# A small first piece of a pooling kernel moved from partitions 0–29 to partitions 64–93

## The chip, the cores and the metric

One core of one Trainium2 chip. The metric is the device time of one execution in microseconds (us). The granted clock was 1.0 throughout. A run also gives a profile of one execution, whose span is about 1.8 us shorter than its time.

## The reference

Pooling with exponent 2 over windows of four along the last axis, float32:

```python
x: (32, 256, 4096), p = 2, kernel_size = 4
result[b, c, i] = sqrt(mean(abs(x[b, c, 4*i : 4*i+4]) ** 2))      # (32, 256, 1024)
```

134.2 MB are read and 33.6 MB written, with one square, three quarters of an add and a quarter of a root per element between. It is a matter of moving data.

## The kernel before

The input is one flat row of numbers. Most of it goes through in 20 big tiles of 128 partitions (up to 13,184 numbers each) in three input slots. ScalarE squares in place, VectorE sums fours into one of two output buffers, ScalarE takes the root, and the result is stored (the last tiles differ a little). What the big tiles do not cover, 840 x 128 numbers, is the small piece: 30 partitions of 3,584 numbers. It is loaded first, into the second output buffer, which is not needed yet.

```python
    Q = 30
    odd = ODD * P // Q                       # 840 * 128 // 30 = 3584
    t = o_tiles[1][0:Q, 0:odd]
    nc.sync.dma_start(out=t, in_=xf[(total - ODD) * P:total * P].rearrange("(p w) -> p w", p=Q))
    ahead = 0
    while ahead < n and loads[ahead][0] < X_SLOTS:
        load(ahead)                          # the first three big tiles, on the same queue
        ahead += 1
    nc.vector.tensor_tensor(out=t, in0=t, in1=t, op=mybir.AluOpType.mult)
    o = o_tiles[1][0:Q, odd:odd + odd // k]
    nc.vector.tensor_reduce(out=o, in_=t.rearrange("p (n j) -> p n j", j=k), ...)
    nc.scalar.activation(out=o, in_=o, func=Act.Sqrt, scale=1.0 / k)
    stores["odd"] = nc.scalar.dma_start(out=..., in_=o)
    ...
    for i in range(n):                       # then tile by tile, shortened
        # load(ahead) as soon as the sums have freed a slot (SyncE's queue)
        # ScalarE: square in place; VectorE: sums; ScalarE: root of an earlier group; store
```

## Time and profile before

| | before |
|---|---|
| median of 3 executions | 393.93 us (393.88 to 394.1) |
| span of the profiled execution | 393.3 us |
| busy, VectorE / ScalarE | 274.5 / 275.4 us (70% each) |
| moved | 167.77 MB, 427 GB/s over the span |

In profile lines ACT is ScalarE and DVE is VectorE; SPq and ACTq are the queues of SyncE and ScalarE, from which loads and stores are issued; xt are the input slots, ot the output buffers.

How to read it: two engines at 70% and data movement at 9 tenths or more in nearly every slice mean that the DMA engines set the time. The lines are in the prediction.

### The profile page before, as it was taken

To read this page: it belongs to the slowest core of one execution; us is meant where nothing else is said; L and a number is where in the kernel's file an instruction comes from. 1 tells how busy PE (TensorE), PEld (TensorE's weight loads), DVE (VectorE), ACT (ScalarE), POOL (GpSimd) and SP (SyncE) were. 2 spreads that over 40 slices of the span, in tenths; PEclk is the share of its full clock that TensorE was granted. 3 is DMA by queue.
4 is the path that set the end of the run, shared out by engine and by line. 5 is a ranking of instruction groups with operands and counts; after the bars stand their busy time and mean duration, and the time that the engine had idled before them with its cause. 6 is when DMAs were issued, how large, how long until landed. Compare 5 with 4: busy or idle time off the path is not lost.

```text
span 393.3 us, 182 instructions
## 1 busy us (share of the span) xinstructions
DVE 274.5 (70%) x36; ACT 275.4 (70%) x38; POOL 0.2 (0%) x4
## 2 busy tenths in 40 slices
DVE  4207898885869376948693869396929690989991
ACT  1095879919990899099809991998099809986991
POOL 0000000000000000000000000000000000000000
DMA  8999999999989999999999999999999899999996
GB/s 312 429 440 429 467 445 451 381 432 469 434 386 429 472 429 429 456 402 429 429 432 426 429 472 429 456 400 467 429 437 429 386 429 467 429 429 423 440 409 295
DMA packets 4554, 167.77 MB, mean 427 GB/s; under 512 B 526, under 2 KB 526, under 8 KB 556
## 3 DMA queue, kind: packets, MB, share of 16 engines
q1 hardware_dynamic: 3501, 144.04, 85.0%
q10 hardware_dynamic: 1053, 23.73, 14.0%
HBM read 134.22 MB, written 33.55 MB: 427 GB/s over the span
## 4 chain that ended last, share of the span: by engine, by line
DMA 54%; ACT 25%; DVE 19%; SPq 0%; issue 0%; ACTq 0%
DMA xt<-in_x_dram 54%; ACT xt L167 22%; DVE ot L111 14%; DVE xt L122 3%; ACT ot L102 3%; DVE ot L124 1%; DVE xt L124 1%; ACT xt L102 1%; SPq L82 0%; ACTq L99 0%; SPq L132 0%
## 5 line engine op out<-in xcount | busy, mean ns | idle before, releaser
L167 ACT ACTIVATE xt<-xt 128x13184 f32<-128x13184 f32 (+4 forms) x23 | 217.4, 9458 | 97.9 <-DMA xt<-in_x_dram 96.2
L111 DVE TENSOR_REDUCE ot<-xt 128x3296 f32<-128x13184 f32 x15 | 208.3, 13886 | 88.7 <-ACT xt L167 88.7
L102 ACT ACTIVATE ot<-ot 128x6592 f32<-128x6592 f32 x9 | 51.1, 5679 | 0.0
L122 DVE TENSOR_TENSOR xt<-xt 128x3296 f32<-128x3296 f32 (+5 forms) x9 | 34.5, 3834 | 16.9 <-ACT xt L167 16.8
L124 DVE TENSOR_TENSOR ot<-xt 128x3296 f32<-128x3296 f32 (+1 forms) x4 | 10.9, 2733 | 0.1
L143 ACT ACTIVATE ot<-ot 30x896 f32<-30x896 f32 x1 | 0.9, 948 | 10.8 <-DVE ot L139 10.8
L137 DVE TENSOR_TENSOR ot<-ot 30x3584 f32<-30x3584 f32 x1 | 3.9, 3880 | 5.0 <-DMA ot<-in_x_dram 5.0
L124 DVE TENSOR_TENSOR xt<-xt 128x1448 f32<-128x1448 f32 (+4 forms) x5 | 7.0, 1409 | 0.2
L102 ACT ACTIVATE xt<-xt 128x3296 f32<-128x3296 f32 (+3 forms) x4 | 5.8, 1445 | 1.1 <-DVE xt L124 1.1
L164 DVE TENSOR_TENSOR xt<-xt 128x5792 f32<-128x5792 f32 x1 | 6.2, 6184 | 0.0
L139 DVE TENSOR_REDUCE ot<-ot 30x896 f32<-30x3584 f32 x1 | 3.9, 3874 | 0.0
L143 ACT ACT_TABLE_LOAD x1 | 1.3, 1283 | 0.7 <-PEq L200 0.7
L200 POOL MEMSET const-bfloat16-1.0<- 128x1 bf16 x1 | 0.1, 101 | 0.0
L200 POOL MEMSET const-uint8-127<- 128x1 uint8 x1 | 0.1, 101 | 0.0
L200 POOL MEMSET const-float32-0.0<- 128x1 f32 x1 | 0.1, 98 | 0.2 <-issue 0.2
L200 POOL MEMSET const-float32-1.0<- 128x1 f32 x1 | 0.1, 98 | 0.0
## 6 DMA issues: line engine op xcount, KB each, us to landing
xt<-in_x_dram SPq DMA_DIRECT2D x19, 6592.0 KB, 31.6
out_dram<-ot ACTq DMA_DIRECT2D x7, 3296.0 KB, 27.4
out_dram<-ot SPq DMA_DIRECT2D x2, 3296.0 KB, 24.0
xt<-in_x_dram SPq DMA_DIRECT2D x1, 5404.0 KB, 24.1
out_dram<-xt SPq DMA_DIRECT2D x1, 1648.0 KB, 11.0
out_dram<-xt SPq DMA_DIRECT2D x1, 1351.0 KB, 6.6
ot<-in_x_dram SPq DMA_DIRECT2D x1, 420.0 KB, 4.2
out_dram<-ot ACTq DMA_DIRECT2D x1, 105.0 KB, 8.7
```

The costliest lines, as they stand in the source:

```text
L102: r = nc.scalar.activation(out=o, in_=o, func=Act.Sqrt, scale=1.0 / k)
L111: r = nc.vector.tensor_reduce(out=o, in_=v.rearrange("p (n j) -> p n j", j=k), axis=mybir.AxisListType.X, op=add,)
L122: r = nc.vector.tensor_tensor(out=h, in0=q[:, :, 0:2], in1=q[:, :, 2:4], op=add)
L124: r = nc.vector.tensor_tensor(out=o, in0=h[:, :, 0], in1=h[:, :, 1], op=add)
L137: nc.vector.tensor_tensor(out=t, in0=t, in1=t, op=mybir.AluOpType.mult)
L139: nc.vector.tensor_reduce(out=o, in_=t.rearrange("p (n j) -> p n j", j=k), axis=mybir.AxisListType.X, op=mybir.AluOpType.add,)
L143: nc.scalar.activation(out=o, in_=o, func=Act.Sqrt, scale=1.0 / k)
L164: r = nc.vector.tensor_tensor(out=v, in0=v, in1=v, op=mybir.AluOpType.mult)
L167: r = nc.scalar.activation(out=v, in_=v, func=Act.Square)
L200: nc = _bacc.Bacc("TRN2", target_bir_lowering=False, num_devices=1)
```

## The change

The intent is to see whether the time depends on which partitions of the on-chip memory the small piece is loaded to. Only its place moves; bytes, instructions and waits stay.

```diff
-    Q = 30
+
+    LOW, Q = 64, 30
     odd = ODD * P // Q
-    t = o_tiles[1][0:Q, 0:odd]
+    t = o_tiles[1][LOW:LOW + Q, 0:odd]
     ...
-    o = o_tiles[1][0:Q, odd:odd + odd // k]
+    o = o_tiles[1][LOW:LOW + Q, odd:odd + odd // k]
```

## The prediction

> **What bounds the kernel now.** I read the page's slices first, then the chain that ended last, then a table of DMA traffic by stage, then the start of the timeline.
>
> Slices of the page (40 equal slices, busy tenths; GB/s moved):
>
> ```profile
> DVE  4207898885869376948693869396929690989991
> ACT  1095879919990899099809991998099809986991
> DMA  8999999999989999999999999999999899999996
> ```
>
> The DMA row is at 9 in nearly every slice, and only the first and the last slice fall clearly short. The two compute engines have 70% each and idle in between. The chain by line says the same:
>
> ```profile
> DMA 54%; ACT 25%; DVE 19%; SPq 0%; issue 0%; ACTq 0%
> DMA xt<-in_x_dram 54%; ACT xt L167 22%; DVE ot L111 14%; DVE xt L122 3%; ACT ot L102 3%; DVE ot L124 1%; DVE xt L124 1%; ACT xt L102 1%; SPq L82 0%; ACTq L99 0%; SPq L132 0%
> ```
>
> It names squares and sums as well, because a load may only be issued when the sums have freed its slot. But a load then takes 30 us and more to land, since two other tiles are queued ahead of it, so the engines that move data are never short of work. By stage (columns: busy us and instructions of each engine, clock, DMA share, GB/s):
>
> ```profile
> 0.00:5.00 5.00, 0.04 (x1) 1.28 (x1) 0.20 (x4) 1.00 0.82 255
> 5.00:13.00 8.00, 7.71 (x2) 0.22 (x1) 0.00 (x0) 1.00 0.98 422
> 94.00:300.00 206.00, 143.07 (x12) 150.03 (x17) 0.00 (x0) 1.00 1.00 434
> 345.00:370.00 25.00, 23.18 (x9) 19.88 (x5) 0.00 (x0) 1.00 1.01 434
> 370.00:394.00 24.00, 14.56 (x8) 14.76 (x7) 0.00 (x0) 1.00 0.84 359
> ```
>
> 434 GB/s is the plateau. The trace's packet records agree: a row of 52,736 B takes 1.947 us at the median, 27.09 GB/s, and 16 of those are 433.4 GB/s. All 167.77 MB at that rate are 387.1 us. The shortfall at the two ends, expressed in time at 434 GB/s, is 5.0 x (434 - 255) / 434 = 2.1 us at the start and 24 x (434 - 359) / 434 = 4.1 us at the end. 387.1 + 2.1 + 4.1 = 393.3 us, which is the span. So only some 6 us of the run are not full-rate traffic, and the change stands in the first 2 of them.
>
> The small piece in the timeline:
>
> ```profile
> 0.73 0.45 SPq L132 DMA_DIRECT2D ot<-in_x_dram  x1
> 1.24 44.83 SPq L82 DMA_DIRECT2D xt<-in_x_dram  x4
> 4.96 3.88 DVE L137 TENSOR_TENSOR ot<-ot 30x3584 f32<-30x3584 f32 x1 [4.96 <-DMA ot<-in_x_dram]
> 8.88 3.87 DVE L139 TENSOR_REDUCE ot<-ot 30x896 f32<-30x3584 f32 x1
> 12.78 0.95 ACT L143 ACTIVATE ot<-ot 30x896 f32<-30x896 f32 x1 [10.77 <-DVE ot L139]
> 13.76 0.64 ACTq L144 DMA_DIRECT2D out_dram<-ot  x1
> 20.60 11.19 ACT L167 ACTIVATE xt<-xt 128x13184 f32<-128x13184 f32 x1 [6.87 <-DMA xt<-in_x_dram]
> 31.82 13.88 DVE L111 TENSOR_REDUCE ot<-xt 128x3296 f32<-128x13184 f32 x1 [19.07 <-ACT xt L167]
> ```
>
> Its arithmetic is finished at 13.73 us, 6.87 us before ScalarE gets the first big tile. What of it lies on the path is only its load, which stands ahead of all the others, and later the traffic of its store.
>
> [...]
> - [...]the piece is held to about half rate: its 30 rows of 14,336 B run from 1.81 to 4.00 us, 430 kB in 2.19 us, 196 GB/s, and a row's median is 0.91 us, 15.8 GB/s, against 27.09 for a row of a big tile.
> - [...]one big row starts at 2.937 us, ahead of the other fifteen (3.2 to 4.0 us).
> [...]
>
> **The change part by part.** The order of instructions on every engine, as built, is the same in both kernels, with the same waits; only the line numbers move. Nothing is added or removed. What moves is the place of two access patterns in the buffer.
> 1. Load of the piece: same 430 kB, same 30 rows[...]. I take 2.19 us again: 0.0 us. ([...]it would take 0.430 MB / 433.4 GB/s = 0.99 us, so 1.2 us is the most that any placement could give here.[...])
> 2. First rows of the big tile. Before, these 16 rows took 2.26 to 2.76 us each and not 1.95, and ended between 5.70 and 6.27 us; the one that started first also ended first. [...] Estimate: +0.1 us, between -0.2 and +0.5.
> 3. Multiply, sum and root on 30 lanes at another start: the same elements per lane, so 3.88 + 3.87 + 0.95 us = 8.70 us as before, and off the path by 6.87 us: 0.0 us.
> 4. Store of the piece: 30 rows of 3,584 B at 0.140 us[...]: 0.0 us.
>
> Sum: 393.93 + 0.1, so I say 394.0 us.
>
> **The rivals.**
> - *The collision at the start becomes a gain.* [...] For it: the 2.1 us at the start are real. [...] At most the 1.2 us of step 1: 392.8 us.
> - *The upper lanes are slower for the compute engines.* Were the 8.70 us doubled, the root would end at 22.4 instead of 13.7 us, and the first square would start 1.8 us late. Nothing in the profile speaks for it. And the first freed slot (at 45.7 us) would come 1.8 us later, while the three tiles queued by then need 3 x 6.75 MB / 433.4 GB/s = 46.7 us from about 3 us on, so until about 50 us: there are 4 us of slack, and the time stays at 394.
> - *A displaced phase persists.* If the engine that led falls behind and keeps its lag through all 20 tiles, each tile lands that much later, but the lag is a constant and not a sum: it is paid once, at most 0.8 us: 394.7 us.
> [...]
>
> **Range and chances.** The known effects lie between -1.2 and +0.8 us; the three runs of before spread over 0.22 us. I put the range at 393.2 to 394.8 us. 2% are 7.9 us, more than all that is not full-rate traffic (6.2 us), so faster by over 2% is nearly ruled out. Slower by over 2% would need a mechanism that the trace does not hint at. Chances: 0.01, 0.98, 0.01.
>
> **What would show it.** Step 1: multiply of the piece starting at 4.96 us, within 0.3. Step 2: first square at 20.60 us, within 0.5. Step 3: 3.88, 3.87 and 0.95 us again. Step 4: store landing in about 8.7 us. The plateau stays at 434 GB/s. I am wrong if the plateau moves, if the first square shifts by more than a microsecond, or if the stage from 94 to 300 us moves fewer bytes.

The sum came to 394.0 us: 393.93 us measured, 0.1 us for step 2 and 0.0 for the three other steps. The 0.1 us of step 2, its bounds, the 0.0 us of steps 1 and 4 and the 0.8 us of the third rival and of the range are no more than estimates. The 1.2 us are an estimate too: the measured 2.19 us of the piece less the 0.99 us that its bytes would need at the 433.4 GB/s of the big rows. Against the first rival it still stands that the bytes are as many, 167.77 MB in both profiles. Where the recorded texts speak of an engine that leads or falls behind, the records show a row or a stream of rows, no more.

## The result, and the profile after

| | before | after |
|---|---|---|
| median | 393.94 us (393.66 to 394.1, 6 executions) | 394.76 us (393.64 to 395.38, 6 executions) |
| ratio | | 1.0018, 95% interval 0.9998 to 1.0037 |
| span of the profiled execution | 393.3 us | 393.6 us |

Ratios are the mean time of one kernel's runs over the mean of the other's in the same rounds, so not quite the ratio of the medians. The verdict is: the same.

Yet the six times after are 395.38, 394.23, 395.33, 395.3, 393.64 and 393.8. They look less like one value with a spread than like two groups, 393.6 to 394.2 us and about 395.3 us. The six of before all lie in the lower one. I call the groups levels and draw the line at 394.5 us; in the executions that came later the upper one proved broad, 394.6 to 395.5 us. Whether the change brings the upper level is the one real question, and the experiments are mostly about it.

The start of the timeline after the change (start us, length us, engine, line, operation; in brackets the idle time before it and what ended it):

```profile
0.73 0.45 SPq L133 DMA_DIRECT2D ot<-in_x_dram  x1
5.07 3.88 DVE L138 TENSOR_TENSOR ot<-ot 30x3584 f32<-30x3584 f32 x1 [5.07 <-DMA ot<-in_x_dram]
8.99 3.88 DVE L140 TENSOR_REDUCE ot<-ot 30x896 f32<-30x3584 f32 x1
12.90 0.94 ACT L144 ACTIVATE ot<-ot 30x896 f32<-30x896 f32 x1 [10.88 <-DVE ot L140]
20.72 11.19 ACT L168 ACTIVATE xt<-xt 128x13184 f32<-128x13184 f32 x1 [6.87 <-DMA xt<-in_x_dram]
```

The three instructions of the piece take 3.88, 3.88 and 0.94 us, against 3.88, 3.87 and 0.95 before. Upper lanes are not slower. Everything is 0.11 to 0.12 us later, from the landing of the piece on. The stages (columns as in the prediction):

```profile
0.00:5.00 5.00, 0.00 (x0) 1.28 (x1) 0.20 (x4) 1.00 0.82 255
5.00:13.00 8.00, 7.76 (x2) 0.10 (x1) 0.00 (x0) 1.00 0.98 422
94.00:300.00 206.00, 143.03 (x12) 149.87 (x17) 0.00 (x0) 1.00 1.00 433
345.00:370.00 25.00, 22.97 (x9) 19.91 (x4) 0.00 (x0) 1.00 1.01 437
370.00:394.00 24.00, 14.82 (x8) 14.99 (x7) 0.00 (x0) 1.00 0.84 359
```

255, 422, 433, 437 and 359 GB/s against 255, 422, 434, 434 and 359: the same stages with the same rates.

### The profile page after: what moved, and what is told of

It is laid out like the page before. It is cut to its first block, busy times and chain, and to the rows that moved or that the text cites. A ratio compares the mean times of both kernels' runs of the same rounds, so it can differ in the third digit from the quotient of the medians.

```text
span 393.6 us, 182 instructions
## 1 busy us (share of the span) xinstructions
DVE 274.5 (70%) x36; ACT 275.4 (70%) x38; POOL 0.2 (0%) x4
## 2 busy tenths in 40 slices
DMA packets 4554, 167.77 MB, mean 426 GB/s; under 512 B 526, under 2 KB 526, under 8 KB 556
## 4 chain that ended last, share of the span: by engine, by line
DMA 54%; ACT 25%; DVE 19%; SPq 0%; issue 0%; ACTq 0%
DMA xt<-in_x_dram 54%; ACT xt L168 22%; DVE ot L111 14%; DVE xt L122 3%; ACT ot L102 3%; DVE ot L124 1%; DVE xt L124 1%; ACT xt L102 1%; SPq L82 0%; ACTq L99 0%; SPq L133 0%
```

## The experiments

Theory A: the placement does not matter, and the two levels come from elsewhere. Theory B: the upper partitions now and then cost something. I worked out the packet numbers below from the trace's packet records, each of which has a start, a duration and a size but not its engine. A row is the run of bytes of one partition and is one packet (30 packets of 14,336 B for the piece, 128 of 52,736 B for each big load, in before and after). Starts and ends of rows are counted from a zero that lies about 0.08 us before that of the timeline.

### 1. The changed kernel again, and the piece in two more places

The changed kernel word for word (again64), and two one-line variants of it. They put the piece on partitions 32 to 61 and 96 to 125.

```diff
-    LOW, Q = 64, 30
+    LOW, Q = 32, 30      # low32
+    LOW, Q = 96, 30      # low96
```

again64. Expected:

> The changed kernel once more, word for word. Theory A (the placement does not matter; the executions near 395.3 us among its first six were the chip's spread): the mean within 0.1% of the kernel before on the same chip, both near 393.9 us, or both with an occasional execution near 395.3. Theory B (the upper partitions cost something now and then): again about half of the executions near 395.3 us, the mean 0.2% above the kernel before, which stays between 393.6 and 394.1.

low32. Expected:

> The piece on partitions 32 to 61: other partitions than the kernel before[...]. Theory A: 393.9 us, within 0.1% of the kernel before. [...] Theory B with the start away from partition 0 as the cause (compute engines or the spread over DMA engines): 394.6 us, some executions near 395.3.

low96. Expected:

> The piece on partitions 96 to 125: other partitions than the changed kernel[...]. Theory A: 393.9 us. Theory B[...]: as the changed kernel, a mean near 394.6 us with some executions near 395.3. In its profile the multiply of the piece should start near 5.07 us as in the changed kernel, against 4.96 before.

| | median (us) | over 394.5 | ratio, 95% interval |
|---|---|---|---|
| before, same chip | 394.63 | 6 of 11 | |
| again64 | 394.41 | 3 of 6 | 0.9999 (0.9981 to 1.0017) |
| low32 | 393.78 | 1 of 6 | 0.9987 (0.9969 to 1.0004) |
| low96 | 393.82 | 2 of 6 | 0.9997 (0.9974 to 1.0019) |

On this chip the kernel before itself reached 395.27 us and had six of eleven executions over 394.5. So the upper level is not the change's. low32 and low96 show it too, in one and two of six executions. Theory B has lost its evidence.

A detail missed: I expected the multiply of low96 to start near 5.07 us. It started at 4.79, and at 4.74 in again64, which is the changed kernel itself. So even the 0.11 us that I saw between the two first profiles is within what one kernel does by itself.

### 2. What the upper level is

Profiles of both levels now existed for the changed kernel. Following the starts of ScalarE's squares through them, the lower one runs within 0.3 us of the upper one until the square near 302 us. Three lines of each, upper level first, the changed kernel's first profile (395.38 us):

```profile
301.62 0.34 ACTq L99 DMA_DIRECT2D out_dram<-ot  x1
302.00 11.19 ACT L168 ACTIVATE xt<-xt 128x13184 f32<-128x13184 f32 x1 [0.42 <-ACT ot L102]
323.72 11.19 ACT L168 ACTIVATE xt<-xt 128x13184 f32<-128x13184 f32 x1 [10.53 <-DMA xt<-in_x_dram]
```

The same kernel's second profile (again64, 393.96 us):

```profile
301.60 0.34 ACTq L99 DMA_DIRECT2D out_dram<-ot  x1
301.98 11.19 ACT L168 ACTIVATE xt<-xt 128x13184 f32<-128x13184 f32 x1 [0.41 <-ACT ot L102]
322.72 11.19 ACT L168 ACTIVATE xt<-xt 128x13184 f32<-128x13184 f32 x1 [9.55 <-DMA xt<-in_x_dram]
```

At 302.0 us the two are 0.02 us apart, and one load later exactly 1.00 us. The kernel before, in the profile on which the prediction rests (395.11 us), has the late landing too, at 323.68. Where it comes from is seen in the rows of the big loads (start of the rows, how many, from the packet records):

```
upper level, kernel before      304.15-304.72: 16   307.07-307.44: 15   307.92: 1   313.28: last of 15   313.83: 1   316.19: last of 15   317.07: 1
upper level, changed kernel     304.09-304.49: 15   304.92: 1   307.01-307.41: 15   307.97: 1   313.25: last of 15   313.99: 1   316.17: last of 15   317.19: 1
lower level, changed kernel     304.34-304.81: 16   307.26-307.76: 16   313.10-313.60: 16                316.01-316.51: 16
```

The records do not name the stream of a row, but rows follow each other at a constant distance (2.9 us in these lines). One of the 16 streams falls behind (whether a stream is one DMA engine is not shown): it takes 2.08 to 2.40 us for some single rows of 52,736 B that take 1.947 us elsewhere, while the other fifteen run on. The square waits for the last row: that row of the load in question ends at 322.44 us in the upper profile and at 321.38 us in the lower one, 1.06 us apart, as the squares are 1.00 us apart. Four more runs tested this on two more copies of each kernel.

same0a (before). Expected:

> The kernel before, word for word, for one more profile and more executions. The two profiles so far that fell near 395.2 us (one of the kernel before, one of the changed kernel) both show one DMA engine of 16 falling 0.5 to 1.3 us behind the others between 302 and 324 us; the profiles near 394.0 show none. Theory S (that straggler is the higher level of the times, whatever the kernel): a profile over 394.5 us shows it again and its square after the one near 302 us starts 21.7 to 21.9 us later; a profile under 394.3 us shows none, and that square comes 20.7 to 20.9 us later. The level is hit by a third to a half of the executions of both kernels.

same64a (changed). Expected:

> The changed kernel, word for word. Theory S: as for the kernel before, by the level of the profiled execution. Theory A: mean within 0.1% of the kernel before. Theory B (the upper partitions cost something): mean 0.2% above the kernel before, as in its first six executions.

same0b (before). Expected:

> The kernel before once more, with the expectations of the first of these four runs.

same64b (changed). Expected:

> The changed kernel once more, with the expectations of the second of these four runs.

| | executions | median (us) | over 394.5 | profiled one | ratio to before, 95% interval |
|---|---|---|---|---|---|
| before, shared | 11 | 394.07 | 3 | | |
| same0a | 6 | 394.94 | 4 | 393.79 | 1.0013 (0.9995 to 1.0031) |
| same0b | 6 | 393.89 | 1 | 394.05 | 0.9998 (0.9981 to 1.0015) |
| same64a | 6 | 394.46 | 3 | 395.27 | 1.0008 (0.9988 to 1.0027) |
| same64b | 5 | 393.89 | 0 | 394.32 | 0.9992 (0.9975 to 1.0008) |

A copy of the kernel before stands at 1.0013 to itself, which is most of the 1.0018 that the change showed at first. In the three profiles on the lower level no stream is more than 0.4 us behind the next between 302 and 324 us. In same0a that square starts at 322.60 us, 20.75 after the one before it:

```profile
301.85 11.19 ACT L167 ACTIVATE xt<-xt 128x13184 f32<-128x13184 f32 x1 [0.42 <-ACT ot L102]
322.60 11.19 ACT L167 ACTIVATE xt<-xt 128x13184 f32<-128x13184 f32 x1 [9.56 <-DMA xt<-in_x_dram]
```

The one on the upper level, same64a, refuted the place that I had named. Its gap there is 20.75 us like the lower ones. It had lost its time before:

```profile
246.22 11.19 ACT L168 ACTIVATE xt<-xt 128x13184 f32<-128x13184 f32 x1 [10.28 <-DMA xt<-in_x_dram]
```

The same square starts at 244.76 to 245.12 us in the lower-level profiles of both kernels, here in same0a:

```profile
244.76 11.19 ACT L167 ACTIVATE xt<-xt 128x13184 f32<-128x13184 f32 x1 [9.55 <-DMA xt<-in_x_dram]
```

In the packet records of same64a one stream was already 0.7 us behind the next when the load before the square at 167.68 us landed, after rows of 2.21 and 2.10 us at about 149 and 158 us. One row near 227.6 us then took 2.68 us instead of 1.95, and from there the last stream stayed 1.3 to 1.5 us behind the next. So in all three upper-level profiles one stream of 16 ends 1.3 us or more behind the next, in both kernels; the losses lie between 149 and 324 us, and the place varies. In the lower-level profiles of the two kernels and of low32 and low96 no big load (13,184 numbers a row) ends with a stream more than 0.4 us behind the next. Executions between the two, such as 394.6 to 395.0 us, were not profiled with either kernel. What holds the stream up is not shown by any run. And since the records name neither stream nor engine, whether it is always the same one stays open as well.

Over all executions of the two kernels, 18 of 51 of the kernel before and 9 of 23 of the changed one lie over 394.5 us. The means are 394.34 and 394.42 us. The difference, 0.08 us, does not stand out from its 95% half-width of 0.33 us (1.96 times the root of the sum of the two variances, each over its number; chips and rounds thrown together).

### 3. Is the piece's load on the path?

The prediction's step 1 says so. Two variants of the changed kernel probe it from both sides: the load made twice, first into the other buffer on partitions 0 to 29 (twice), and the load spread over 128 partitions (q128).

```diff
+    nc.sync.dma_start(out=o_tiles[0][0:Q, 0:odd], in_=<the same piece>)       # twice: a line ahead
     nc.sync.dma_start(out=t, in_=<the piece>)
```
```diff
-    LOW, Q = 64, 30
+    LOW, Q = 0, 128      # q128: 128 rows of 840 numbers
```

twice. Expected:

> The changed kernel with the load of the piece made twice, first to partitions 0 to 29 of the other output buffer[...], then to 64 to 93[...]: 430 kB more at the head of the queue. If the load of the piece is on the path at its half rate: 2.2 us more, 396.1 us. If only its bytes count: 0.43 MB / 433.4 GB/s = 1.0 us more, 394.9 us, and the first square at 21.6 us. If the load is hidden: 393.9 us.

q128. Expected:

> The piece as 128 rows of 3,360 B over all partitions[...]. My estimate of the most that a placement can give was 1.2 us. If the half rate of the piece is what lies on the path, the first square starts about 1.2 us earlier (19.4 us instead of 20.6) and the time is 392.7 us. If it is hidden (the later rows use what the piece leaves idle), 393.9 us. The multiply, sum and root of the piece shrink from 8.7 us to about 3 us, which should change nothing.

twice: 396.13 us (395.87 to 396.29, six executions), 1.0042 of before (1.0026 to 1.0058). Its timeline:

```profile
7.09 3.88 DVE L139 TENSOR_TENSOR ot<-ot 30x3584 f32<-30x3584 f32 x1 [7.09 <-DMA ot<-in_x_dram]
22.70 11.19 ACT L169 ACTIVATE xt<-xt 128x13184 f32<-128x13184 f32 x1 [6.84 <-DMA xt<-in_x_dram]
```

The first square is 2.0 us later than in the changed kernel's first profile, and the median 2.1 us above that of before on the same chip. The packet records have the doubled piece from 1.81 to 6.06 us: 860 kB in 4.25 us, 202 GB/s. One load to partitions 0 to 29 and the next to 64 to 93 did not overlap to any gain. So the second load at the head of the queue was paid at its own half rate, about 2 us (2.0 in the first square, 2.1 in the medians) and not the 1.0 us of its bytes at full rate. The ratio alone would not show it: its interval is about 1.0 to 2.3 us, since the runs of before lie on two levels.

q128: 394.90 us (394.03 to 395.09, six), 1.0005 of before (0.9990 to 1.0021); the 392.7 us did not come.

```profile
4.11 1.03 DVE L138 TENSOR_TENSOR ot<-ot 128x840 f32<-128x840 f32 x1 [4.11 <-DMA ot<-in_x_dram]
20.22 11.19 ACT L168 ACTIVATE xt<-xt 128x13184 f32<-128x13184 f32 x1 [13.60 <-DMA xt<-in_x_dram]
```

Its rows of 3,360 B run at 0.132 us at the median, 25.5 GB/s, so the half rate of a row is gone. But the first square comes only 0.3 to 0.5 us earlier than in the changed kernel's profiles (20.48 to 20.76), not 1.2. Fifteen of the first big rows end at 5.14 to 5.78 us, against 5.65 to 6.37 for all sixteen in the changed kernel; the sixteenth ends at 6.13. I overlooked why the gain is so small: from the first row to the last the spread piece still took 2.0 us (1.79 to 3.83), not the 0.99 us that its bytes need at full rate, since early rows took up to 0.68 us each. Against 2.34 us in the changed kernel's first profile that saves 0.3 us of the piece's own time. And even that lead is lost: the fourth square starts at 68.70 us, against 68.84 in again64, and the fifth at 89.22 us, against 89.04. Between the two, the rows that start at 69.9 to 70.6 us took 2.32 to 2.89 us each, and in again64 1.95 to 2.71. Why they stretch more here is open. Timed against each other, a smoother start is not worth anything that these runs can show. Five of the six executions lie at 394.7 to 395.1 us; none of these was profiled, so what they lost is not shown.

### 4. The load beside the big loads

```diff
-    nc.sync.dma_start(out=t, in_=<the piece>)
+    nc.scalar.dma_start(out=t, in_=<the piece>)      # on_act
```

> The load of the piece is issued by ScalarE's queue, so it no longer stands ahead of the big loads but beside them. The bytes are the same. If its half rate at the head of the queue costs the 1.2 us that I put down as the most: 392.7 us. If the total of bytes is what counts: 393.9 us, with the multiply of the piece later than 5.07 us and the first square no more than 0.5 us from 20.6 us.

A clear miss: 396.58 us (396.17 to 397.1, six), 1.0056 of before (1.0039 to 1.0072), 2.6 us above its median of 394.02. The big load is issued at once, and still lands later:

```profile
13.16 3.88 DVE L138 TENSOR_TENSOR ot<-ot 30x3584 f32<-30x3584 f32 x1 [13.16 <-DMA ot<-in_x_dram]
22.90 11.19 ACT L168 ACTIVATE xt<-xt 128x13184 f32<-128x13184 f32 x1 [0.97 <-DMA xt<-in_x_dram]
```

In the packet records the piece's rows go in between the first, second and third rows of the big tile: at 4.33 to 5.59 us and 7.81 to 9.61 us. They stay below the 27.09 GB/s of a big row there (0.77 us at the median, 18.6 GB/s), and the big rows that start at 8.0 to 10.5 us took 2.20 to 3.38 us. So the piece is not hidden behind the big load. It holds up the big rows beside it, and somewhat more than at the head of the queue, where the first big rows took 2.21 to 2.65 us in the changed kernel.

### 5. How much the start can take

Spare multiplies of the piece delay its root, and so the first square, which follows it on ScalarE.

```diff
+    spare = o_tiles[0][LOW:LOW + Q, 0:odd]
+    for _ in range(2):                               # extra2; 5 in extra5
+        nc.vector.tensor_tensor(out=spare, in0=t, in1=t, op=mybir.AluOpType.mult)
     nc.vector.tensor_tensor(out=t, in0=t, in1=t, op=mybir.AluOpType.mult)
```

extra2. Expected:

> The changed kernel with two more multiplies of the piece into an unused place: 2 x 3.88 = 7.8 us more VectorE work on the piece before its root. Theory A (8.70 us of lane work lie off the path, with some 4 us of slack behind it): the root of the piece ends near 21.6 us, the first square starts about 1 us later than 20.7 us, the first freed slot comes about 1 us later (46.8 us), still before the three queued tiles are through (50 us), and the time stays within 0.3 us of the kernel before. Rival (anything that delays the first square is paid at the end): 0.9 to 1.2 us slower.

extra5. Expected:

> Five more multiplies: 19.4 us more. The root ends near 33.2 us, so the first square starts 12.6 us late and the first slot is freed near 58.3 us, 8 to 9 us after the three queued tiles are through. Theory A with its 4 us of slack: the engines that move data run dry from about 50 to 59 us, and the time rises by 8 to 9 us, to 402 to 403 us (faster by 0.98, a control that the start can hurt when the slack is spent). Rival (the later slack of 6.9 us before each square takes it up): under 400 us.

extra2: 394.63 us (394.17 to 395.77, six), 1.0008 of before (0.9990 to 1.0027).

```profile
22.30 11.19 ACT L171 ACTIVATE xt<-xt 128x13184 f32<-128x13184 f32 x1 [0.70 <-ACT ot L147]
36.60 11.19 ACT L171 ACTIVATE xt<-xt 128x13184 f32<-128x13184 f32 x1 [3.10 <-DMA xt<-in_x_dram]
```

The first square is 1.6 us later than in the changed kernel's first profile (20.72; I had expected about 1), the second 0.3 us later (36.28), and the last root starts at 384.50 us, against 384.23 in again64. The delay is absorbed, as the prediction's second rival said that it would be if the upper lanes were slower. The median is still 0.6 us above that of before on the same chip, but some 0.4 us of this lie outside the span: the times of extra2 exceed their spans by 2.1 to 2.2 us, those of before by 1.8. The medians of the spans are 392.45 and 392.2 us. What takes time outside the span is not shown.

extra5: 405.98 us (405.52 to 406.43, five), 1.0296 of before (1.0276 to 1.0316), where I expected 402 to 403. Its stages:

```profile
44.00:54.00 10.00, 8.78 (x1) 10.00 (x2) 0.00 (x0) 1.00 0.59 253
54.00:64.00 10.00, 10.00 (x2) 10.00 (x2) 0.00 (x0) 1.00 0.47 169
```

The data movement runs dry here as expected, and the traffic missing in the two stages is 10 x (434 - 253) / 434 + 10 x (434 - 169) / 434 = 10.3 us. The first slot was freed at 59.1 us (45.22 + 13.89, the first sum), and the rows that then start at 60.2 to 60.8 us took 2.2 to 3.6 us each: the traffic that started anew here was slow at first. I had counted the gap and not that. The remaining 1 to 2 us come mostly next: the fourth square starts 10.2 us later than in again64 (79.08 against 68.84 us), the fifth 11.2 us later (100.22 against 89.04), and the last root 11.4 us later (395.65 against 384.23). What slows the load between the fourth and the fifth square is not shown.

## Why the prediction was right, point by point

- **The bound and the plateau.** Right. The plateau stays at 432 to 434 GB/s with the piece anywhere (94 to 300 us in the profiles of before, after, again64, low32, low96 and q128), and no variant that kept its bytes was faster than before beyond the noise.
- **Step 1, the load.** Right for this change: the piece ran from 1.81 to 4.15 us after, from 1.81 to 4.00 before, at 1.80 to 4.03 in again64. That such a load stands on the path is shown by the load made twice. The side estimate that a full spread could give 1.2 us was too high: it took all of the time above 0.99 us for half rate, but the spread piece still took 2.0 us; the first square gained 0.3 to 0.5 us and the end nothing.
- **Step 2, the first rows.** The size held, a reason failed: that the row that leads would lose its lead. The first square started at 20.54 to 20.60 us in three profiles of before and at 20.48 to 20.76 in four of the changed kernel, means 20.56 and 20.68: the +0.1 us that I put down, though within the spread. But the row stream that leads did not lose it, as far as records without names can tell: after the change the earliest big row ended at 5.65 us and the next at 5.95, against 5.70 and 5.89 before. (In same64a no row starts ahead of the rest, yet one still ends at 5.78 us and the next at 6.10.)
- **Step 3, the lanes.** Right: 8.70 us in both.
- **Step 4, the store.** Right: 8.7 us to landing in the two first profiles. (In again64 it was 7.1 us, with nothing gained: it is off the path.)
- **The rivals.** The gain at the start did not come; the fourth stays open, since the packet records name no engine (the piece ends with 15 packets of 4 B in before and after, and with 16 in q128); slower lanes did not show (8.70 us in both), and of the 4 us of slack claimed for them extra2 shows 1.6 us. A displaced phase of one row stream does exist, but not where I put it: it starts far into the run (149 us or later), in some executions of either kernel, and costs about 1.3 us.
- **The range.** It held with 0.04 us to spare, and partly by luck: a median of six executions over two levels falls where the draw puts it. I took the spread from three executions of before, all on the lower level, and overlooked that the profiled one, 395.11 us, was on the upper. Single executions of both kernels go up to about 395.5 us. For the same reason the sum 387.1 + 2.1 + 4.1 = 393.3 us fits that span better than it should: with the rates of again64 (255 and 358 GB/s at the ends) it gives 393.4 us, for a span of 392.2. Such a sum is good to a microsecond, no better. And 1.7 us of the start pass before the first row starts: at 1.71 to 1.74 us on the timeline in every profile, wherever the piece goes.

## What to carry to other kernels

When data movement is at its plateau from start to end, look for what lies outside the plateau before moving anything: here some 6 us of 394, and moving the piece to other partitions did not measurably change even those (1.0018, 0.9998 to 1.0037). A difference of 0.2% needs the kernel timed against itself: a copy of before stood at 1.0013, and executions of one kernel fell on two levels, their medians 1.3 us apart. When a median wanders, take a profile on each level and follow one engine's starts until they part.
